# A third pair of up tiles by products of quarters, first in each of the last three passes of the MLP

## Chip, cores and metric

The kernel runs on 1 core of one Trainium2 chip. The metric is the device time of one execution in microseconds (us), as the median of several runs.

## The reference

Two decoder layers on a float32 input of 512 tokens by 1024 features. Each layer adds a mixer (four token mixers on one normalised input, gated and projected) and then an MLP:

```
for l in range(DEPTH):                       # DEPTH = 2
    h = rms_norm(x, ln_mix[l])
    x = x + hybrid_mixer(h, ...)             # not touched here
    h = rms_norm(x, ln_mlp[l])
    x = x + square(relu(h @ w_up[l])) @ w_down[l]   # 1024 -> 4096 -> 1024
```

## The kernel before

All products are float32 products made of three TensorE matmuls (`mm3`, line 268): each operand is split into a rounded part (`hi`) and the rest (`lo`), and hi·hi, hi·lo and lo·hi are added in PSUM. Activations are split once per layer. Weights come from one packed array in DRAM and are split as they arrive (`split_w`, line 258): ScalarE writes `whi`, VectorE writes `wlo`, into three rotating buffers each, so that a split may run three uses ahead of the matmuls.

The **MLP** (`mlp`, line 389) runs once per layer. Its 32 tiles of 128 columns of `w_up` are worked in four **passes** of eight (`PASSES`). In a pass, `t` runs from 0 to 3; each `t` makes one **pair** of up tiles, 256 hidden columns for all 512 tokens. A pair is made in one of two ways:

- **plain**: two weight tiles of 128x1024 through `next_w` (one load of 512 KB into a `raw` buffer, of which there are two, one split), each multiplied with all tokens: 2 tiles x 8 steps x 3 = 48 matmuls of 512 columns, into two PSUM banks of the kind `mm`;
- **by quarters** (`up_seven`, line 417), for the `t` listed in `SEVEN` for the pass: the pair is treated as a 2x2 block product, made with seven block products in place of eight (Winograd's form of Strassen's scheme). Four quarter weights B11, B12, B22, B21 of 256 KB each are loaded by SyncE's queue (line 426) into halves of four `cr` buffers; VectorE forms S1w = B11 + B12, S2w = S1w + B22, S3w = B12 + B22 and all4 = S2w + B21 in other halves of them; the four buffers `R[0..3]` are split as one each; then 7 forms x 4 steps x 3 = 84 matmuls of 256 columns go into four PSUM banks of the kind `ms`, in the order A, B, C, E, with small sums and copies between the forms. The sums of the activations (`sh`, `sl`) are made once per layer.

After each pair, ScalarE and VectorE form seven combinations of it (`ah`, `al`) for the second half of the pass, the **down products**, which are by quarters too: two groups of banks, `A`, `B` of the kind `mm` and `C`, `E` of the kind `ms` (E is ms2 and ms3). Their order on TensorE is A11 and S1, then S2, S4 (by k), S3, and at the end A22 and A12 by turns for k = 0, 1: A22 goes to E, A12 to A. When A22 of k = 1 is done, VectorE takes E out (`c21`, lines 708 to 713, two subtractions of 512 columns into `co`), while TensorE does the last A12. `turn.update(mm=2, ms=2)` (line 637) sets which banks come next: the next plain pair begins with mm2, the next pair by quarters with ms2.

The **six `cr` buffers** (`CRB`) serve the quarters of both halves: `chain` (2, W11 + W12 of the down weights, held to the end of the pass), `b22` (2) and `sum2` (2) in the down products, and four for each pair by quarters. A buffer goes to the next claimant when its last reader is done, so the quarters of the next pass are loaded while the down products still run. In passes 0 to 2 the results are added up in DRAM (`keep`), by SyncE's queue in pass 0 and by GpSimd's after it.

Nothing is ordered by hand beyond this. A scheduler puts the instructions of each engine in a fixed order before the run, by priority (weights and evictions are raised above the rest) and by its own estimate of when each is ready. On the chip each engine takes its instructions in that order.

Of the kernel before, what the change touches and what calls it, by code (L numbers as in the profile page):

```python
# [34 lines left out]
G1K = ((1, 1, 2, 2, 2), (2, 2, 2, 2))  # L35
KORD = ((0, 1, 2, 3, 4, 5, 6, 7), (4, 5, 6, 7, 0, 1, 2, 3))
PASSES = (8, 8, 8, 8)
SEVEN = ((2, 3), (2, 3), (2, 3), (2,))
CRB = 6
BIG = 1e30  # L40

# [12 lines left out]
def chunk_plan(l):  # L54
# [30 lines left out]
    for p, nt in enumerate(PASSES):  # L85

        half = nt // 2 * P
        for t in range(0, half, P):
            parts = 2 if t // P in SEVEN[p] else 1
            for i in range(parts):  # L90
# [80 lines left out]
def trunk(tc, x_in, wall, consts, lps, sgus, out):  # L171
# [5 lines left out]
    with ExitStack() as es:  # L177
# [14 lines left out]
        def mmtile(name, tag="mm", bank=None):  # L192
            if bank is None:
                bank = turn[tag]
                turn[tag] = (bank + 1) % 4
            return psum.tile([P, 512], F32, name=name, tag=f"{tag}{bank}")
# [49 lines left out]
        def next_w(raw=None):  # L246
            kk, n = chunk_shape(plan[pos[0]])
            pos[0] += 1
            L = kk * n
            if raw is None:  # L250
                raw = wpool.tile([P, WCH], F32, name="raw", tag="raw", bufs=WB[0])
            src = wall[off[0]:off[0] + P * L].rearrange("(p l) -> p l", l=L)
            off[0] += P * L
            with HP():
                nc.sync.dma_start(raw[:, :L], src)
            return split_w(raw, L, n, V.tensor_copy if pos[0] == 1 else S.copy)

        def split_w(raw, L, n, copy=S.copy):
            hi = wpool.tile([P, WCH], F32R, name="whi", tag="whi", bufs=WB[1])
            lo = wpool.tile([P, WCH], F32R, name="wlo", tag="wlo", bufs=WB[1])  # L260
            with HP():
                copy(hi[:, :L], raw[:, :L])
                r = V.tensor_sub(lo[:, :L], raw[:, :L], hi[:, :L].bitcast(F32))
            at["first"] = r if pos[0] == 1 else None
            return (hi[:, :L].rearrange("p (k n) -> p k n", n=n),
                    lo[:, :L].rearrange("p (k n) -> p k n", n=n))

        def mm3(o, ah, al, bh, bl, start, stop, more=False):

            T_.matmul(o, ah, bh, start=start, stop=False, skip_group_check=more)  # L270
            T_.matmul(o, ah, bl, start=False, stop=False, skip_group_check=more)
            r = T_.matmul(o, al, bh, start=False, stop=stop, skip_group_check=more)
            if not at["side"]:
                at["mm"] = r
# [11 lines left out]
        def tick():  # L286
            at["side"] = True
            for g in list(side):
                if next(g, side) is side:
                    side.remove(g)  # L290
            at["side"] = False
# [97 lines left out]
        def mlp(l, hh, hl, r2, gain, fp, sh, sl):  # L389
# [10 lines left out]
            with tc.tile_pool(name="ap", bufs=1) as ap:  # L400
                def ftile(name, tag):
                    return ap.tile([P, 7, 256], F32R, name=name, tag=tag)
# [4 lines left out]
                def cr():  # L407
                    return ap.tile([P, 1024], F32, name="cr", tag="cr", bufs=CRB)

                def moving(f, k):  # L410

                    if f >= S3:
                        return sh[k][:, f - S3], sl[k][:, f - S3]
                    k, r = k + 4 * (f in (A22, A12)), (row2, row1)[f in (A11, A12)]
                    return hh[k][:, r], hl[k][:, r]

                def up_seven(F):

                    base, sz = off[0], P * 512
                    off[0] += 4 * sz  # L420
                    pos[0] += 4

                    def ld(dst, i, j):
                        o = base + ((i - 1) * 2 + j - 1) * sz
                        with HP():
                            nc.sync.dma_start(dst, wall[o:o + sz].rearrange("(p l) -> p l", l=512))

                    R = [cr() for _ in range(4)]
                    R[1:] = R[2:] + R[1:2]
                    lo, up = slice(0, 512), slice(512, 1024)  # L430
                    B11, S1w, S2w, B22 = R[0][:, lo], R[0][:, up], R[1][:, lo], R[1][:, up]
                    S3w, all4, B21, B12 = R[2][:, lo], R[2][:, up], R[3][:, lo], R[3][:, up]
                    ld(B11, 1, 1)
                    ld(B12, 1, 2)
                    ld(B22, 2, 2)
                    ld(B21, 2, 1)
                    sums = {0: ((S1w, B11, B12),), 1: ((S2w, S1w, B22),), 2: ((S3w, B12, B22), (all4, S2w, B21)), 3: ()}
                    ws = [None] * 4

                    def form(f, o, i, n, first=True):  # L440
                        if ws[i] is None:
                            for o_, a_, b_ in sums[i]:
                                with HP():
                                    V.tensor_add(o_, a_, b_)
                            ws[i] = split_w(R[i], 512 if i == 3 else 1024, P)
                        w_h, w_l = ws[i]
                        for k in range(4):
                            bh, bl = moving(f, k)
                            mm3(o, w_h[:, 4 * n + k], w_l[:, 4 * n + k], bh, bl, first and k == 0, k == 3, not first)
                        tick()  # L450

                    A, B, C, E = (mmtile("up", "ms")[:, 0:256] for _ in range(4))
                    s1, s2 = (hpool.tile([P, 2, 256], F32, name="U", tag=n) for n in ("acc", "sq"))
                    U, U2, W, R5 = s1[:, 0], s1[:, 1], s2[:, 0], s2[:, 1]
                    form(A11, A, 0, 0)
                    with HP():
                        S.copy(U, A)
                    form(S1, B, 0, 1)
                    with HP():
                        S.copy(R5, B)  # L460
                    form(S2, C, 1, 0)
                    with HP():
                        V.tensor_sub(U2, C, U)
                    form(S4, B, 1, 1, False)
                    with HP():
                        V.tensor_add(F[:, A12], B, U2)
                    form(S3, C, 2, 0, False)
                    with HP():
                        V.tensor_sub(W, C, U)
                        V.tensor_add(F[:, A22], W, R5)  # L470
                        S.activation(F[:, 2:4], F[:, 2:4], AF.Relu)
                    form(A22, E, 2, 1)
                    with HP():
                        V.tensor_sub(F[:, A21], E, W)
                        S.activation(F[:, A21], F[:, A21], AF.Relu)
                    form(A12, A, 3, 0, False)
                    with HP():
                        S.activation(F[:, A11], A, AF.Relu)
                        S.activation(F, F, AF.Square)

                for p, nt in enumerate(PASSES):
                    nk = nt // 2
                    ah, al = [], []
                    for t in range(nk):
                        F = ap.tile([P, 4, 256], F32, name="F", tag="F")
                        G_ = ap.tile([P, 4, 256], F32, name="Fs", tag="Fs")
                        ah.append(ftile("ah", f"ah{t}"))
                        al.append(ftile("al", f"al{t}"))
                        if t == 1:
                            early = at["mm"]  # L490
                        if t in SEVEN[p]:
                            up_seven(F)
                        for i in range(0 if t in SEVEN[p] else 2):
                            w_h, w_l = next_w()
                            pt = mmtile("up")
                            fm_group(pt, w_h, w_l, hh, hl)
                            a = flat(F[:, 2 * i:2 * i + 2])
                            with HP():
                                S.activation(a, pt, AF.Relu)
                                S.activation(a, a, AF.Square)  # L500
                        with HP():
                            S.copy(ah[t][:, 0:3], F[:, 1:4])
                            V.tensor_sub(G_[:, 0:2], F[:, A21:A21 + 1].to_broadcast([P, 2, 256]), F[:, A11:A22 + 1])
                            V.tensor_sub(G_[:, 2], F[:, A11], G_[:, 1])
                            V.tensor_sub(G_[:, 3], F[:, A12], G_[:, 2])
                            S.copy(ah[t][:, 3:7], G_)
                            V.tensor_sub(al[t][:, 0:3], F[:, 1:4], ah[t][:, 0:3].bitcast(F32))
                            V.tensor_sub(al[t][:, 3:7], G_, ah[t][:, 3:7].bitcast(F32))
# [1096 lines left out]
```

## Time and profile before

| | us |
|---|---|
| median of 3 runs | 1582.65 (1582.23 to 1583.69) |
| the profiled execution, its own time | 1581.15 |
| its span, first to last instruction | 1579.4 |
| TensorE busy in the span | 1571.7 |
| VectorE busy | 1220.8 |
| ScalarE busy | 754.6 |

In the profile PE is TensorE's matmuls, PEld its weight loads, DVE is VectorE, ACT is ScalarE, POOL is GpSimd, SP is SyncE's queue. Times of rows are us from the span's start. Matmuls overlap in their pipeline: the step from one start to the next is what a matmul costs, and not the duration in its row. The granted clock is 1.0 of full speed in all slices of the span. The first layer's MLP runs from 461 to about 790 us, the second's from 1246 to the end.

### The profile page before, as it was taken

The numbers are of one execution on the slowest core, as the hardware profiler recorded it, in microseconds if no ns is written. First come the engines' busy times: TensorE is split into PE (matmuls) and PEld (weight loads), VectorE is DVE, ScalarE is ACT, GpSimd is POOL, SyncE is SP. The second block draws the span as 40 slices with busy tenths as digits, with TensorE's granted clock in tenths as the row PEclk, the third lists the DMA queues.
The fourth block names the chain that finished last, engine by engine and source line by source line (L and its number), as shares of the span: only waits on it lengthen the run. The fifth ranks groups of instructions, "written<-read, shape, count | busy, mean of one in ns | idle before, by whom it ended". The sixth has DMA issues, their size and how long they took to land.

```text
span 1579.4 us, 21779 instructions
## 1 busy us (share of the span) xinstructions
PE 1571.7 (100%) x8091; PEld 1319.1 (84%) x8091; DVE 1220.8 (77%) x2103; ACT 754.6 (48%) x1164; POOL 144.7 (9%) x189
## 2 busy tenths in 40 slices
PE   9999999999999999999999999999999999999998
PEld 8888888888888898988888888887888898989887
DVE  6899997645588787775978999975555896868677
ACT  5553224423356464746645433254233574737463
POOL 1322000000001011111013120000000010111110
PEclk9999999999999999999999999999999999999999
DMA  7533322332346466769445232223223565576692
GB/s 194 144 92 111 102 90 95 103 115 91 106 157 196 161 179 132 201 140 271 130 130 141 86 118 95 86 99 137 83 98 113 167 165 181 162 166 181 147 280 81
DMA packets 77835, 218.22 MB, mean 138 GB/s; under 512 B 8832, under 2 KB 16192, under 8 KB 77728
## 3 DMA queue, kind: packets, MB, share of 16 engines
q1 hardware_dynamic: 60784, 175.54, 33.8%
q0 software_dynamic: 16080, 40.27, 13.2%
q8 instruction: 64, 1.05, 0.3%
q10 hardware_dynamic: 864, 1.01, 0.2%
q14 instruction: 43, 0.35, 0.1%
HBM read 192.10 MB, written 21.01 MB: 135 GB/s over the span
## 4 chain that ended last, share of the span: by engine, by line
PE 91%; DVE 5%; DMA 2%; issue 1%; ACT 1%; SPq 0%; POOL 0%; DVEq 0%; ACTq 0%; POOLq 0%
PE g L143 21%; PE up L143 20%; PE tk L143 10%; PE q L143 10%; PE fm L143 8%; PE r L143 6%; PE p L143 5%; PE wo L143 4%; DVE wlo L143 2%; DMA cr<-in_wall_dram 1%; PE ix L143 1%; PE lg L143 1%; PE av L143 1%; PE pT L143 1%; DVE cr L143 0%
## 5 line engine op out<-in xcount | busy, mean ns | idle before, releaser
L143 ACT CAST whi<-raw 128x1024 fp32r<-128x1024 f32 (+3 forms) x208 | 228.6, 1099 | 217.4 <-DMA raw<-in_wall_dram 89.7
L143 DVE TENSOR_TENSOR wlo<-raw,whi 128x1024 fp32r<-128x1024 f32 (+3 forms) x209 | 267.8, 1282 | 80.0 <-ACT whi L143 79.6
L143 PE MATMUL g<-hh,whi 128*128 128x512 f32 x512 | 200.7, 392 | 0.0
L143 PE MATMUL g<-hh,wlo 128*128 128x512 f32 x512 | 199.7, 390 | 0.0
L143 PE MATMUL g<-hl,whi 128*128 128x512 f32 x512 | 199.5, 390 | 0.0
L143 DVE TENSOR_TENSOR wlo<-cr,whi 128x1024 fp32r<-128x1024 f32 (+1 forms) x136 | 157.8, 1165 | 45.1 <-ACT whi L143 44.9
L143 ACT CAST whi<-cr 128x1024 fp32r<-128x1024 f32 (+1 forms) x136 | 136.0, 1006 | 93.5 <-PE up L143 38.6
L143 PE MATMUL up<-hh,whi 128*128 128x512 f32 (+1 forms) x456 | 160.6, 352 | 0.0
L143 PE MATMUL up<-hh,wlo 128*128 128x512 f32 (+1 forms) x456 | 160.0, 351 | 0.4 <-DVE wlo L143 0.3
L143 PE MATMUL up<-hl,whi 128*128 128x512 f32 (+1 forms) x456 | 159.8, 350 | 0.0
L143 ACT ACTIVATE gs<-gs 128x512 f32<-128x512 f32 x64 | 40.6, 634 | 199.4 <-DVE gs L143 199.2
L143 PEld LDWEIGHTS g<-hh,wlo 128*128 128x128 f32 x512 | 96.1, 188 | 20.3
L143 PEld LDWEIGHTS g<-hh,whi 128*128 128x128 f32 x512 | 96.2, 188 | 19.5
L143 PEld LDWEIGHTS g<-hl,whi 128*128 128x128 f32 x512 | 96.2, 188 | 19.4
L143 PE MATMUL tk<-whi,hh 128*128 128x512 f32 (+2 forms) x304 | 107.9, 358 | 0.0
L143 PE MATMUL tk<-wlo,hh 128*128 128x512 f32 (+2 forms) x304 | 107.0, 354 | 0.2 <-DVE wlo L143 0.2
L143 PE MATMUL tk<-whi,hl 128*128 128x512 f32 (+2 forms) x304 | 106.5, 353 | 0.0
L143 DVE TENSOR_TENSOR gs<-g,rb 128x512 f32<-128x512 f32 x64 | 44.0, 688 | 78.8 <-PE g L143 78.7
L143 PE MATMUL q<-whi,ah 128*128 128x512 f32 (+1 forms) x260 | 100.5, 390 | 0.0
L143 PE MATMUL q<-whi,al 128*128 128x512 f32 (+1 forms) x260 | 100.0, 390 | 0.0
L143 PE MATMUL q<-wlo,ah 128*128 128x512 f32 (+1 forms) x260 | 99.6, 387 | 0.0
L143 PEld LDWEIGHTS up<-hh,wlo 128*128 128x128 f32 x456 | 86.3, 189 | 12.5 <-DVE wlo L143 1.3
(310 smaller groups left out, 3550.6 us busy)
## 6 DMA issues: line engine op xcount, KB each, us to landing
raw<-in_wall_dram SPq DMA_DIRECT2D x135, 512.0 KB, 3.7
raw<-in_wall_dram SPq DMA_DIRECT2D x64, 640.0 KB, 3.9
cr<-in_wall_dram POOLq DMA_DIRECT2D x48, 512.0 KB, 8.2
cr<-in_wall_dram SPq DMA_DIRECT2D x32, 512.0 KB, 5.1
cr<-in_wall_dram SPq DMA_DIRECT2D x56, 256.0 KB, 2.9
sum_dram<-co POOLq DMA_DIRECT2D x32, 256.0 KB, 5.8
x<-in_x_dram SPq DMA_DIRECT2D x16, 256.0 KB, 4.8
xm_dram<-x SPq DMA_DIRECT2D x16, 256.0 KB, 2.0
```

The costliest lines, as they stand in the source:

```text
L143: r = f(*a, **k)
```

## The change

```diff
-SEVEN = ((2, 3), (2, 3), (2, 3), (2,))
+SEVEN = ((2, 3), (0, 2, 3), (0, 2, 3), (0, 2))
...
-                def up_seven(F):
+                def up_seven(F, first):
...
                     R = [cr() for _ in range(4)]
-                    R[1:] = R[2:] + R[1:2]
+
+                    R = [R[2], R[0], R[1], R[3]] if first else [R[0], R[2], R[3], R[1]]
...
                         if t in SEVEN[p]:
-                            up_seven(F)
+                            up_seven(F, t == 0)
```

In passes 1, 2 and 3 of both layers the pair `t` = 0 is made by quarters in place of plain: six pairs in all. For these six the four `cr` buffers take other parts: of the four in the order in which they are claimed, the third holds B11 and S1w, the first S2w and B22, the second S3w and all4, the fourth B21 and B12. For all other pairs by quarters the parts are as before: first B11 and S1w, second B21 and B12, third S2w and B22, fourth S3w and all4. The packing of the weights follows `SEVEN`, so the DRAM array holds the four quarters of these pairs one after another. The bytes loaded per pair are the same, 1 MB.

## Rows read from the trace of the kernel before

**Rows 1.** The page: busy time of the engines with share of the span and count, and the chain of work that ended last, by engine.

```profile
PE 1571.7 (100%) x8091; PEld 1319.1 (84%) x8091; DVE 1220.8 (77%) x2103; ACT 754.6 (48%) x1164; POOL 144.7 (9%) x189
PE 91%; DVE 5%; DMA 2%; issue 1%; ACT 1%; SPq 0%; POOL 0%; DVEq 0%; ACTq 0%; POOLq 0%
```

**Rows 2.** Timeline of PE, layer 0, pass 3: the first matmul of the plain pairs 0 and 1, of the pair by quarters, of the plain pair behind it, and of the down products. Columns: start us, duration us, engine, line, operation, output and operands, shape.

```profile
705.03 0.39 PE L143 MATMUL up<-hh,whi 128*128 128x512 f32 x1
...
726.79 0.28 PE L143 MATMUL up<-hh,whi 128*128 128x256 f32 x1
726.91 0.28 PE L143 MATMUL up<-hl,whi 128*128 128x256 f32 x1
727.03 0.28 PE L143 MATMUL up<-hh,wlo 128*128 128x256 f32 x1
...
736.87 0.40 PE L143 MATMUL up<-hh,whi 128*128 128x512 f32 x1
737.10 0.40 PE L143 MATMUL up<-hl,whi 128*128 128x512 f32 x1
...
747.77 0.39 PE L143 MATMUL q<-whi,ah 128*128 128x512 f32 x1
```

**Rows 3.** The same starts in layer 1, pass 3.

```profile
1488.81 0.39 PE L143 MATMUL up<-hh,whi 128*128 128x512 f32 x1
...
1510.57 0.28 PE L143 MATMUL up<-hh,whi 128*128 128x256 f32 x1
...
1520.64 0.40 PE L143 MATMUL up<-hh,whi 128*128 128x512 f32 x1
```

**Rows 4.** Timeline of PE at the head of pass 2 (layer 0, then layer 1): the first three matmuls of the plain pair 0, and the first of the pair by quarters that ends the two plain pairs; the bracket is idle time before the instruction and its releaser.

```profile
623.94 0.39 PE L143 MATMUL up<-hh,whi 128*128 128x512 f32 x1
624.17 0.39 PE L143 MATMUL up<-hl,whi 128*128 128x512 f32 x1
624.89 0.50 PE L143 MATMUL up<-hh,wlo 128*128 128x512 f32 x1 [0.33 <-DVE wlo L143]
...
646.35 0.28 PE L143 MATMUL up<-hh,whi 128*128 128x256 f32 x1
...
1407.93 0.39 PE L143 MATMUL up<-hh,whi 128*128 128x512 f32 x1
...
1430.13 0.28 PE L143 MATMUL up<-hh,whi 128*128 128x256 f32 x1
```

**Rows 5.** Groups of instructions by shape while TensorE works on the pair by quarters of pass 3, layer 0 (726.79 to 736.87 us): count, busy us, mean ns of one. Neighbouring work of the engines is among them.

```profile
L143 DVE TENSOR_TENSOR wlo<-raw,whi 128x1024 fp32r<-128x1024 f32 x2 | 2.4, 1221 | 0.3 <-ACT whi L143 0.3
L143 ACT CAST whi<-raw 128x1024 fp32r<-128x1024 f32 x2 | 2.1, 1052 | 2.0 <-PE up L143 2.0
L143 DVE TENSOR_TENSOR U<-up,U 128x256 f32<-128x256 f32 x2 | 0.8, 418 | 0.0
L143 DVE TENSOR_TENSOR F<-up,U 128x256 f32<-128x256 f32 x2 | 0.8, 416 | 0.0
L143 DVE TENSOR_TENSOR wlo<-cr,whi 128x512 fp32r<-128x512 f32 x1 | 0.7, 683 | 0.0
L143 DVE TENSOR_TENSOR F<-U 128x256 f32<-128x256 f32 x1 | 0.4, 424 | 0.0
```

**Rows 6.** Busy time of the engines by stage, layer 0: down products of pass 1, then pass 2: the two plain pairs, the two pairs by quarters, the down products. Columns: stretch, its us, then busy us (count) of PE, PEld, DVE, ACT, POOL, granted clock, mean busy share of the DMA engines, GB/s.

```profile
585.65:623.94 38.29, 38.29 (x170) 31.40 (x169) 31.12 (x36) 18.85 (x23) 4.29 (x5) 1.00 0.66 161
623.94:646.35 22.41, 22.08 (x98) 17.95 (x96) 12.35 (x15) 11.40 (x16) 3.46 (x4) 1.00 0.65 153
646.35:666.73 20.38, 20.38 (x170) 20.21 (x168) 18.84 (x30) 15.24 (x23) 3.82 (x6) 1.00 0.76 201
666.73:705.03 38.30, 38.30 (x170) 31.40 (x169) 32.73 (x38) 20.07 (x25) 5.91 (x7) 1.00 0.64 154
```

**Rows 7.** Timeline of DVE around the head of pass 2, layer 0 (the pass begins at 623.94): sums of the next pass's quarters (cr<-cr), splits (wlo), and the two subtractions that take E out (co<-r,Z).

```profile
607.07 1.22 DVE L143 TENSOR_TENSOR wlo<-cr,whi 128x1024 fp32r<-128x1024 f32 x1
...
610.05 1.89 DVE L143 TENSOR_TENSOR cr<-cr 128x512 f32<-128x512 f32 x3
...
615.39 1.22 DVE L143 TENSOR_TENSOR wlo<-cr,whi 128x1024 fp32r<-128x1024 f32 x1
617.07 1.23 DVE L143 TENSOR_TENSOR wlo<-raw,whi 128x1024 fp32r<-128x1024 f32 x1 [0.46 <-ACT whi L143]
623.00 0.69 DVE L143 TENSOR_TENSOR cr<-cr 128x512 f32<-128x512 f32 x1 [4.71 <-DMA cr<-in_wall_dram]
623.61 1.22 DVE L143 TENSOR_TENSOR wlo<-raw,whi 128x1024 fp32r<-128x1024 f32 x1
624.75 1.28 DVE L143 TENSOR_TENSOR co<-r,Z 128x512 f32<-128x512 f32 x2
```

**Rows 8.** The same place in layer 1, and at the head of pass 1 in layer 0 and layer 1 (these begin at 543.51 and 1327.51), E's subtractions and the sum before them.

```profile
1406.77 0.69 DVE L143 TENSOR_TENSOR cr<-cr 128x512 f32<-128x512 f32 x1 [4.49 <-DMA cr<-in_wall_dram]
...
1408.52 1.28 DVE L143 TENSOR_TENSOR co<-r,Z 128x512 f32<-128x512 f32 x2
...
541.46 0.69 DVE L143 TENSOR_TENSOR cr<-cr 128x512 f32<-128x512 f32 x1 [3.60 <-DMA cr<-in_wall_dram]
543.21 1.28 DVE L143 TENSOR_TENSOR co<-r,Z 128x512 f32<-128x512 f32 x2
...
1323.42 0.69 DVE L143 TENSOR_TENSOR cr<-cr 128x512 f32<-128x512 f32 x1 [1.55 <-DMA cr<-in_wall_dram]
...
1325.16 1.28 DVE L143 TENSOR_TENSOR co<-r,Z 128x512 f32<-128x512 f32 x2
```

**Rows 9.** Timeline of DVE at the head of pass 3, layer 0 (it begins at 705.03): no sum of quarters stands there.

```profile
698.16 1.22 DVE L143 TENSOR_TENSOR wlo<-raw,whi 128x1024 fp32r<-128x1024 f32 x1 [0.46 <-ACT whi L143]
700.88 1.22 DVE L143 TENSOR_TENSOR wlo<-raw,whi 128x1024 fp32r<-128x1024 f32 x1 [1.50 <-ACT whi L143]
702.02 1.28 DVE L143 TENSOR_TENSOR co<-r,Z 128x512 f32<-128x512 f32 x2
```

**Rows 10.** SP's queue: the loads of quarters during the down products of pass 1, layer 0; and, over the whole run, from issue to landing of these loads.

```profile
597.70 0.33 SPq L426 DMA_DIRECT2D cr<-in_wall_dram  x1
602.36 8.13 SPq L426 DMA_DIRECT2D cr<-in_wall_dram  x4
...
616.64 0.83 SPq L426 DMA_DIRECT2D cr<-in_wall_dram  x2
DMA to landing us min/median/max: 2.4/2.9/8.2
```

## The prediction

> **What bounds the kernel now.** I read the page first. TensorE is busy for 1571.7 of the span's 1579.4 us and carries 91% of the chain that ended last; VectorE follows with 77%, ScalarE with 48% [rows 1]. A chain of that kind is shortened by taking matmul time away, if nothing new keeps TensorE waiting. A busy matmul row is not yet a price, since matmuls overlap, so next I read starts in TensorE's timeline: from the head of a pair to the head of the next one [rows 2, 3]. Then the heads of the passes, where the change puts its work: TensorE's waits there [rows 4], what VectorE has in hand [rows 7 to 9], and what loads run [rows 10]. Last, busy time by stage, for whether VectorE can carry the new work [rows 6].
>
> **What is removed and added on TensorE.** A plain pair costs (726.79 - 705.03) / 2 = 10.88 us, that is 48 steps of 0.227 [rows 2]. A pair by quarters between plain ones costs 736.87 - 726.79 = 10.08 us, 84 steps of 0.120 [rows 2]; in layer 1 it is (1510.57 - 1488.81) / 2 = 10.88 against 10.07 [rows 3]. So a quarter step is more than half a plain step, and of the eighth of the columns that the scheme saves (84 x 256 against 48 x 512) only 0.80 us of 10.88 is left. The new pair also has a plain pair behind it, so I take the 10.08. Six pairs: 6 x 0.80 = **4.8 us less**, 0.30% of the run.
>
> **VectorE, ScalarE.** A plain pair asks VectorE for two splits, 2 x 1.22 = 2.4 us. A pair by quarters asks for four sums of 0.69 (the row at 623.00 in [rows 7]), three splits of 1.22, one of 0.68, and five small operations of 0.42 [rows 5]: 2.8 + 4.3 + 2.1 = 9.2. So each new pair adds 6.8 us to VectorE. On the path it would be ruinous. I cost it at nothing, since this is its cover: in pass 2 VectorE is busy 12.35 of 22.41 us in the two plain pairs and 18.84 of 20.38 in those by quarters [rows 6]; with 6.8 more, 38.0 of about 42, still under the time, and part of it (sums, the first split) falls into the down products before, where 31.12 of 38.29 are used. If that cover is gone, the price is the overhang of VectorE over TensorE. ScalarE, at 11.40 of 22.41 [rows 6], gets 1.7 casts of 1.05 [rows 5] and some small copies: nothing. The quarters' own evictions run in the existing pairs without a wait that I can see in their 10.08 us.
>
> **Loads and queues.** Two loads of 512 KB become four of 256 KB on SP's queue: the same bytes, two more issues of 0.33 [rows 10]. What matters is when buffers come free. The loads of quarters in pass 1's down products start at 597.70, four from 602.36 to 610.5, and two at 616.64 [rows 10]: I read this as the first pair by quarters getting the buffers of b22 and sum2, which are done early, and the second one those of chain, of which the last is held by the split at 615.39 to 616.61 [rows 7]. After the change the new pair gets the early four. With its exchanged parts, its sums wait for the fourth, freed when the split at 607.07 ends, about 608.3 [rows 7]; with the median landing of 2.9 us [rows 10] they can start at about 611.2, and the first split is wanted at 623.94, 12 us later. With the longest landing, 8.2, it is still 7 us early. I cost this at nothing. On SP, what waits behind these loads are the raw loads of the pair after (needed 10 us later than today) and in pass 0 the stores of sums, which nobody waits for. GpSimd's queue is passed by nothing.
>
> **The heads of the passes: what goes and what comes.** Today the head of pass 2 loses 22.41 - 21.76 = 0.65 us in layer 0 and (1430.13 - 1407.93) - 21.76 = 0.44 in layer 1: the third matmul waits for a wlo [rows 4], and that is late because VectorE stood 4.71 us before a sum whose quarter had not landed, with the ready split behind it [rows 7]. This sum belongs to the second pair by quarters of the coming pass, 22 us before its use.
>
> The change adds one wait here. The plain pair begins in bank mm2; the new pair begins in ms2, which is half of E. Its first form cannot start before VectorE's first subtraction on E is over; behind that form stands the whole of TensorE. Undisturbed, that subtraction is early: at pass 3 the two run from 702.02 to 703.30, the first done at about 702.66, 2.4 us before the head [rows 9]. Behind a stalled sum it is late: 624.75 + 0.64 = 625.39, 1.45 after the head of pass 2; 1408.52 + 0.64 is 1.23 after it in layer 1; in pass 1 0.35 after it in layer 0 (543.85), and 1.7 before it in layer 1 (1325.80) [rows 7, 8]. No row shows pass 3 with such a sum: bounds 0 [rows 9] and 1.45 [rows 7].
>
> Does the stalled sum still stand ahead of E's subtraction? The next pair in line for the two late buffers is then `t` = 2, so a sum of the same kind can stand there, its load issued at the same moment. But that order is the scheduler's, by its estimate of readiness, and VectorE now has the new pair's four sums, which come earlier in the program and so take precedence, in the same stretch (from 611 on, where three such sums stood at 610.05 [rows 7]); E's subtraction also takes precedence over the stray sum once both are ready. I hold it a little likelier that the sum falls behind. Bounds of the new waits together: 0, and 5.7 if all is as today (0.35 + 1.45 + 0 + 1.23, and 2 x 1.34 for pass 3, the mean of 1.45 and 1.23). I take 0.7, two heads at the smallest late row, being nearer to the undisturbed row.
>
> The row at 623.00 shows VectorE idle with ready work behind a blocked instruction. The Trainium skill, PSUM — Partial Sum Buffer, section Engine vs sequencer instructions, says that ScalarE's and VectorE's queues are strictly first in, first out, and this row agrees. The rule speaks against the change: by it any late quarter ahead of E's subtraction holds TensorE itself, which is the second case below; by the sum above it would not.
>
> **The sum.** Old stalls gone 1.1, matmul time 4.8, new waits 0.7: 5.2 us less. Against the profiled execution, 1581.15 - 5.2 = 1575.95; the median of three runs stands 1.5 us above that execution, so on it 1582.65 - 5.2 = **1577.5**. What the measurement can tell from no change is about 0.2%, or 3.2 us.
>
> **The rivals.**
> 1. *Forecast.* E is out before the head in most passes. With new waits of 0 to 2.7 us: 1576.7 to 1579.4. Chance 0.48.
> 2. *The wait moves instead of going.* The stray sum stays ahead of E's subtraction; the 5.7 us of waits above replace the 1.1 and eat the gain: 1582.65 - 5.9 + 5.7 = **1582.4**, from 1579.5 to 1585 as landings vary. For it: four heads of four have the sum ahead today (541.46, 623.00, 1323.42, 1406.77 [rows 7, 8]). Against it: the fuller VectorE. Chance 0.35.
> 3. *Slower.* One mechanism, same place: at the heads the first form waits for E, E's subtraction for a sum, the sum for a quarter that lands later than today, since the new pair's loads are in flight too. The landing of 623.00 was 6.3 us after its issue at 616.64; the longest in the run is 8.2 [rows 10], so a head can lose 1.45 + 1.9 = 3.35 us, and six lose 20: 1597. It makes the kernel slower from (5.9 + 3.2) / 6 = 1.5 us a head; at 2.5 a head it gives 1582.65 - 5.9 + 15 = **1591.8**. Against it: the DMA engines' mean share there is 0.65 [rows 6], and the bytes are the same. Chance 0.14.
> 4. *The short matmuls run at half the plain step.* Then the pair costs 84 x 0.1134 = 9.52 and six save 8.2: 1582.65 - 8.2 - 0.4 = **1574.0**. The rows speak against it, 0.120 in both layers [rows 2, 3]. Chance 0.03. The Trainium skill, TensorE: Matmul & The Clock Gate, section Back-to-back issue gap, gives N/2.4 + 2.5 ns for a lone warm matmul, 109 ns at 256 columns and 216 at 512; an estimate by that page would save 1.2 us a pair, 7.1 in all. The trace differs, 120 and 227, and decides.
>
> That the change does not do what it says is no case: `SEVEN` alone chooses, and matmuls of 256 columns must grow by 6 x 84.
>
> **How the numbers follow.** Predicted is the first case. The range takes in cases 1 and 2 nearly whole, from 1576.2 (no new wait, less the 0.4 us by which the lowest run lies below the median) to 1584.5; outside lie case 3, case 4 and a little of case 2. Faster by over 0.2% (under 1579.5): cases 1 and 4 and a little of 2, 0.53. Slower (over 1585.8): case 3 and a shade more, 0.15. Within: 0.32. The forecast's own range is 1576.2 to 1579.4.
>
> **What would show it.** Right: `t` = 0 of passes 1 to 3 takes 10.1 us from its first to the next pair's first matmul; E's subtractions end before the heads; no wait of TensorE there. Case 2 or 3: the first matmul of 256 columns in a pass starts 0.3 to 3 us late with VectorE's co as releaser, and VectorE waits for cr from DMA ahead of it. If `t` = 0 is longer without a late start, VectorE has no room and the cover above was wrong. If waits appear in pairs 2 and 3, the exchange of buffers has made their loads late, which I have costed at nothing.

## The result and the profile after

The changed kernel is slower: 1596.18 us median (1593.51 to 1598.97, 4 runs) against 1582.67 (4 runs), a ratio of 1.0082 with a 95% interval of 1.0068 to 1.0097. The profiled execution took 1595.87 us with a span of 1594.1, both 14.7 us more than before (1581.15 and 1579.4). Forecast was 1577.5 in a range up to 1584.5; the time lies outside, where the prediction had put a chance of 0.15.

The page of the changed kernel, busy time and chain by engine, beside [rows 1]:

```profile
PE 1572.3 (99%) x8307; PEld 1326.3 (83%) x8307; DVE 1259.0 (79%) x2169; ACT 766.9 (48%) x1188; POOL 145.1 (9%) x189
PE 72%; DVE 12%; issue 6%; DMA 6%; ACT 2%; POOL 1%; SPq 0%; DVEq 0%; ACTq 0%; POOLq 0%
```

PE is still 99% busy by that row. What changed is the chain: TensorE carries 72% of it in place of 91, VectorE 12 in place of 5, DMA 6 in place of 2. So I read where TensorE waited. Waits of PE over the whole span, in total, times, longest:

```profile
PE up L143 <- ACT U L143: 4.9, 5, 1.3
PE up L143 <- DVE co L143: 4.0, 3, 2.1
PE up L143 <- DVE wlo L143: 3.1, 2, 1.9
PE up L143 <- ACT whi L143: 2.3, 2, 1.2
```

That is 14.3 us. The same view of the kernel before has only two rows of up tiles, 0.9 us in all, the first of them in pass 0:

```profile
PE up L143 <- DVE U L143: 0.6, 1, 0.6
PE up L143 <- DVE wlo L143: 0.3, 1, 0.3
```

The new waits lie at three places of a pass. Timeline of PE of the changed kernel, layer 0, pass 2: the first form of the new pair, its fourth form, the plain pair 1, and a stretch behind it; then the heads of pass 1 and 3 in layer 0, and of pass 1 in layer 1.

```profile
626.39 0.36 PE L143 MATMUL up<-hh,whi 128*128 128x256 f32 x1 [1.14 <-ACT whi L143]
...
632.21 0.39 PE L143 MATMUL up<-sh,whi 128*128 128x256 f32 x1 [1.27 <-ACT U L143]
...
640.54 0.50 PE L143 MATMUL up<-hh,wlo 128*128 128x512 f32 x1 [1.85 <-DVE wlo L143]
...
642.99 0.63 PE L143 MATMUL up<-hh,whi 128*128 128x512 f32 x1
643.41 0.63 PE L143 MATMUL up<-hl,whi 128*128 128x512 f32 x1
...
544.70 0.36 PE L143 MATMUL up<-hh,whi 128*128 128x256 f32 x1 [0.32 <-DVE co L143]
...
713.12 0.36 PE L143 MATMUL up<-hh,whi 128*128 128x256 f32 x1 [1.54 <-DVE co L143]
...
1337.15 0.28 PE L143 MATMUL up<-hh,whi 128*128 128x256 f32 x1
...
1347.23 0.40 PE L143 MATMUL up<-hh,whi 128*128 128x512 f32 x1
```

Undisturbed, in pass 1 of layer 1, the new pair takes 1347.23 - 1337.15 = 10.08 us, the forecast price of [rows 2]. Elsewhere it is late. The table goes by the starts of neighbouring matmuls in the same view (a start less the start before it, less one step):

| place | us late, layer 0 passes 1, 2, 3 | layer 1 | sum |
|---|---|---|---|
| first form of the new pair | 0.48, 1.29, 1.69 | 0, 1.33, 2.27 | 7.1 |
| fourth form (S4), with slow steps around it | 0.7, 1.5, 1.4 | 0, 1.4, 1.4 | 6.4 |
| plain pair 1 | 0, 3.8, 0 | 0, 1.5, 0 | 5.3 |
| slow steps at heads, start of pass 3's down products | | | 1.5 |

That is 20.3 us; with 4.8 saved on matmuls and 1.1 of old waits gone, it makes 14.4 beside the 14.7 us measured. Two differences outside these places are not in that sum and cancel in part: the first up matmul starts 1.5 us later (462.98 in place of 461.44), and 0.8 us is gone with the wait in pass 0.

VectorE of the changed kernel at the head of pass 2, layer 0, to set against [rows 7], and on into pair 1 (on time the pass would begin at 625.10, which is 626.39 less the 1.29 of the table):

```profile
618.22 1.23 DVE L143 TENSOR_TENSOR wlo<-raw,whi 128x1024 fp32r<-128x1024 f32 x1 [0.45 <-ACT whi L143]
623.82 0.69 DVE L143 TENSOR_TENSOR cr<-cr 128x512 f32<-128x512 f32 x1 [4.37 <-DMA cr<-in_wall_dram]
624.43 1.22 DVE L143 TENSOR_TENSOR wlo<-cr,whi 128x1024 fp32r<-128x1024 f32 x1
625.57 1.28 DVE L143 TENSOR_TENSOR co<-r,Z 128x512 f32<-128x512 f32 x2
626.76 1.21 DVE L143 TENSOR_TENSOR wlo<-cr,whi 128x1024 fp32r<-128x1024 f32 x1
628.37 1.90 DVE L143 TENSOR_TENSOR cr<-cr 128x512 f32<-128x512 f32 x3 [0.39 <-DMA cr<-in_wall_dram]
...
638.33 0.69 DVE L143 TENSOR_TENSOR cr<-cr 128x512 f32<-128x512 f32 x1 [3.96 <-DMA cr<-in_wall_dram]
638.94 0.42 DVE L143 TENSOR_TENSOR U<-up,U 128x256 f32<-128x256 f32 x1
639.27 1.22 DVE L143 TENSOR_TENSOR wlo<-raw,whi 128x1024 fp32r<-128x1024 f32 x1
```

The stray sum, that of a later pair, is still there (623.82), for pair 2, with 4.37 us of idle time before it. E's first subtraction ends at about 625.57 + 0.64 = 626.21 and the first form starts at 626.39, though PE's row names ScalarE's whi: the cast that ended last before it (625.29 + 1.04 = 626.33, next view) is of a split that the first form does not read; its own was cast at 619.85. At the heads where no cast falls there (544.70, 713.12 above) the row names VectorE's co. A second stray sum, for pair 3, stands at 638.33 ahead of the split that pair 1 wants; TensorE's matmul of 640.54 comes behind that split.

ScalarE of the changed kernel at the same place: casts, the two evictions of the last down product (co<-q), and the copies (U<-up) that the fourth form needs.

```profile
619.85 1.05 ACT L143 CAST whi<-cr 128x1024 fp32r<-128x1024 f32 x1 [1.67 <-PE q L143]
...
623.93 0.59 ACT L143 COPY co<-q 128x512 f32<-128x512 f32 x1 [0.30 <-PE q L143]
625.29 1.04 ACT L143 CAST whi<-cr 128x1024 fp32r<-128x1024 f32 x1 [0.77 <-PE q L143]
630.51 0.59 ACT L143 COPY co<-q 128x512 f32<-128x512 f32 x1 [4.17 <-DMA sum_dram<-co]
630.99 0.38 ACT L143 COPY U<-up 128x256 f32<-128x256 f32 x1
...
631.77 0.39 ACT L143 COPY U<-up 128x256 f32<-128x256 f32 x1
```

The second eviction waits 4.17 us for its result buffer, until an earlier result has been stored; the two copies stand behind it, and the fourth form starts at 632.21 when the second copy is over. With three buffers that earlier result is E's first half, whose store starts when its subtraction is done. In the kernel before the same eviction waited for a store too, with no matmul behind it that needed such copies:

```profile
631.44 0.59 ACT L143 COPY co<-q 128x512 f32<-128x512 f32 x1 [2.17 <-DMA sum_dram<-co]
```

### The profile page after: what moved, and what is told of

Read it like the earlier page. It is cut to its first block, busy times and chain, and to the rows that moved or that the text cites. A ratio compares the mean times of both kernels' runs of the same rounds, so it can differ in the third digit from the quotient of the medians.

```text
span 1594.1 us, 22365 instructions
## 1 busy us (share of the span) xinstructions
PE 1572.3 (99%) x8307; PEld 1326.3 (83%) x8307; DVE 1259.0 (79%) x2169; ACT 766.9 (48%) x1188; POOL 145.1 (9%) x189
## 4 chain that ended last, share of the span: by engine, by line
PE 72%; DVE 12%; issue 6%; DMA 6%; ACT 2%; POOL 1%; SPq 0%; DVEq 0%; ACTq 0%; POOLq 0%
PE g L143 17%; PE up L143 15%; PE tk L143 8%; PE q L143 8%; PE fm L143 6%; PE wo L143 5%; PE p L143 4%; PE r L143 4%; DVE wlo L143 4%; DMA cr<-in_wall_dram 3%; DVE sco L143 2%; DMA raw<-in_wall_dram 2%; ACT whi L143 1%; DMA sum_dram<-co 1%; DVE m L143 1%
## 5 line engine op out<-in xcount | busy, mean ns | idle before, releaser
L143 ACT CAST whi<-raw 128x1024 fp32r<-128x1024 f32 (+3 forms) x196 | 215.8, 1102 | 173.7 <-DMA raw<-in_wall_dram 36.5
L143 DVE TENSOR_TENSOR wlo<-raw,whi 128x1024 fp32r<-128x1024 f32 (+3 forms) x197 | 253.0, 1285 | 34.3 <-ACT whi L143 33.1
L143 ACT CAST whi<-cr 128x1024 fp32r<-128x1024 f32 (+1 forms) x160 | 158.7, 997 | 114.6 <-PE r L143 43.7
L143 DVE TENSOR_TENSOR wlo<-cr,whi 128x1024 fp32r<-128x1024 f32 (+1 forms) x160 | 183.7, 1153 | 37.4 <-ACT whi L143 36.9
L143 PE MATMUL up<-hh,whi 128*128 128x256 f32 (+1 forms) x432 | 144.6, 335 | 6.3 <-DVE co L143 4.0
L143 PE MATMUL up<-hh,wlo 128*128 128x256 f32 (+1 forms) x432 | 143.5, 332 | 3.1 <-DVE wlo L143 3.1
L143 PE MATMUL up<-hl,whi 128*128 128x256 f32 (+1 forms) x432 | 143.2, 332 | 0.0
L143 PEld LDWEIGHTS g<-hh,wlo 128*128 128x128 f32 x512 | 96.1, 188 | 20.3
L143 DVE TENSOR_TENSOR cr<-cr 128x512 f32<-128x512 f32 (+1 forms) x96 | 71.8, 776 | 47.7 <-DMA cr<-in_wall_dram 47.4
```

Source lines behind the costliest of these rows:

```text
L143: r = f(*a, **k)
```

## The experiments

My theory after this reading is one cause: in VectorE's fixed order the sums of later pairs stand ahead of urgent work and wait for quarters that land late; ScalarE's delay follows from E's late exit. The rivals are that VectorE has no room for the new pair, the claim on E's bank, the result buffer, and the place at the head. Open besides is what makes the quarters late. Ratios are to the kernel before as run beside each experiment (medians 1583.2 to 1583.5).

**e1: both stray sums held back.**

```diff
-    V.tensor_add(o_, a_, b_)
+    r = V.tensor_add(o_, a_, b_)
+if gate is not None:     # order for the scheduler alone
+    tc.add_manual_dep(ins_of(r), ins_of(gate).name, V._dep, reason="pace")
...
+    heads.append(at["mm"])          # last matmul before pair t
-    up_seven(F, t == 0)
+    up_seven(F, t == 0, heads[t - 2] if t > 1 else None)
```

> The changed kernel, with one ordering rule for the scheduler: the sums of quarters of pair 2 come only after the last matmul of the pass before, those of pair 3 only after the last matmul of pair 0. Loads, splits, banks and matmuls are as in the changed kernel. My theory: in the fixed order of VectorE a sum of a later pair stands ahead of work that TensorE needs now, at the head of the pass (the sum at 623.82) and again in the plain pair 1 (the sum at 638.33), and waits there for a quarter that lands late; ScalarE's late copies at the head are a consequence (E's results leave late, so their stores end late and the last eviction of the down products waits for its buffer). Then nearly all of the 20 us of waits goes: 1576 to 1580 us. Rival, VectorE has no room: the same work in another order still takes as long, 1592 or more. Rival, the bank: E's half is claimed too early whatever VectorE's order, 1588 or more.

Measured: 1580.45 us (10 runs), ratio to before 0.9977 (0.9968 to 0.9987). VectorE in this run at the head of pass 2, layer 0:

```profile
621.41 1.23 DVE L143 TENSOR_TENSOR wlo<-cr,whi 128x1024 fp32r<-128x1024 f32 x1 [1.50 <-ACT whi L143]
622.55 1.28 DVE L143 TENSOR_TENSOR co<-r,Z 128x512 f32<-128x512 f32 x2
624.13 1.22 DVE L143 TENSOR_TENSOR wlo<-cr,whi 128x1024 fp32r<-128x1024 f32 x1 [0.29 <-ACT whi L143]
625.27 0.68 DVE L143 TENSOR_TENSOR cr<-cr 128x512 f32<-128x512 f32 x1
626.59 1.29 DVE L143 TENSOR_TENSOR cr<-cr 128x512 f32<-128x512 f32 x2 [0.63 <-DMA cr<-in_wall_dram]
```

The pass begins on time at 625.56, and E's first subtraction starts 3.0 us ahead of that; in the changed kernel it started 0.5 us behind it (625.57 against 625.10). Of the waits in the new pairs and in pair 1 only the fourth form's are left, 0.4, 0.5, 1.3 and 0.4 us. The time is 0.45 us above the range that I had given. The same operations in another order take 16 us less, so VectorE has the room; the order was the cause of most of it. The bank's rival falls too: E's half is still claimed first. But ScalarE's delay does not follow from E's late exit alone: 2.5 us of it stay with E on time, and e5 removes them.

**e2: only pair 2's sums held back** (`heads[0] if t == 2 else None`).

> As the run before, but only the sums of pair 2 are held back; the early sum of pair 3 stays where it is. My theory: the waits at the heads and at the fourth form (about 14 us) go, those in pair 1 of the two passes with three pairs by quarters (about 5 us with the slower clock behind one of them) stay: 1580 to 1586 us. If the waits in pair 1 came only from the late heads, they go as well and the time is that of the run before.

Measured: 1583.05 us (10 runs), ratio 0.9994 (0.9984 to 1.0003). The late matmul of pair 1 in pass 2, layer 0 and then layer 1:

```profile
636.78 0.50 PE L143 MATMUL up<-hh,wlo 128*128 128x512 f32 x1 [1.16 <-DVE wlo L143]
...
1419.90 0.50 PE L143 MATMUL up<-hh,wlo 128*128 128x512 f32 x1 [0.41 <-DVE wlo L143]
```

By starts it is late by 1.33 us in layer 0 and 0.57 in layer 1; in the changed kernel pair 1 lost 3.8 and 1.5. So the sum of pair 3 is a cause of its own, about 2 us here (the medians of e2 and e1 lie 2.6 apart), and the larger part of what pair 1 lost, the slower clock behind it included, goes with the sums of pair 2.

**e3: another bank.**

```diff
-turn.update(mm=2, ms=2)
+turn.update(mm=2, ms=0 if p < last else 2)
```

> The changed kernel with one number changed: in passes 0 to 2 the next pair by quarters begins with bank ms0 (free since the product S3) in place of ms2 (half of E). Nothing else moves. If the claim on E's bank is the cause, the 7 us of late heads go and the fourth form is on time: 1585 to 1590 us. My theory: the third matmul of the first form then waits for the first split, which stands behind the same stalled sum and ends only 0.6 us before E's first subtraction does, and the later waits stay: 1592 to 1596 us.

Measured: 1598.02 us (4 runs), ratio 1.0088 (1.0073 to 1.0103): nothing gained, and 2 us above the range of my theory. PE at the head of pass 2, layer 0, and at the fourth form:

```profile
624.00 0.28 PE L143 MATMUL up<-hh,whi 128*128 128x256 f32 x1
...
624.98 0.39 PE L143 MATMUL up<-hh,wlo 128*128 128x256 f32 x1 [0.58 <-DVE wlo L143]
...
631.48 0.39 PE L143 MATMUL up<-sh,whi 128*128 128x256 f32 x1 [2.16 <-ACT U L143]
```

The first matmul is on time, the third waits for the split behind the stray sum (late by 0.74, 0.95, 0.94, 1.59 us in passes 2 and 3), and the fourth form, late by 1.3 or 1.4 us before, is late by 2.0 to 2.4. The wait that I had forecast, E's bank, was only the first of several in a row on the same late sum.

**e4: a fourth result buffer.**

```diff
-n = at["co"] = (at["co"] + 1) % 3
+n = at["co"] = (at["co"] + 1) % 4
...
```

> The changed kernel with a fourth result buffer for the down products (three before), and a narrower table of constants that makes room for it. The last eviction by ScalarE then need not wait for a store, so the copies behind it that the fourth form needs are early. Heads and pair 1 are untouched. If ScalarE's wait is a cause by itself, 5 to 6 us go: 1589 to 1592 us. If something else is just as late there (VectorE's split of the second buffer, at 627.97), the gain is 0 to 2 us: 1594 to 1597.

Measured: 1594.91 us (4 runs), ratio 1.0070 (1.0053 to 1.0088). Pair 1 of pass 2, layer 0:

```profile
640.89 0.63 PE L143 MATMUL up<-hh,wlo 128*128 128x512 f32 x1 [2.81 <-DVE wlo L143]
```

The waits for ScalarE's copies are gone (the fourth form is late by at most 0.4 us), yet this matmul of pair 1 is now late by 2.97 and 3.00 us in the two layers. Counted from the head's due time it starts about 15.5 us later in both kernels (640.54 - 625.10; 640.89 - 625.42). What is saved ahead of a stray sum is lost at it.

**e5: sums held back and the fourth buffer** (e1 and e4 together).

> Both pairs' sums held back as in the first experiment, and the fourth result buffer. What is left in the first experiment are waits of the fourth form for ScalarE's copy (0.4, 0.4, 1.3, 0.3 us) that stands behind the eviction of the down products, which waits for its buffer. If that is all, they go: 1577 to 1579 us, the new pair takes 10.1 to 10.2 us at all six places. If the fourth form then waits for something else as late, the time stays at 1580.

Measured: 1578.49 us (1577.68 to 1579.72, 6 runs), ratio 0.9966 (0.9954 to 0.9979). Timeline of PE in this run, pass 2, layer 0, the first matmul of the new pair and of pair 1:

```profile
624.50 0.28 PE L143 MATMUL up<-hh,whi 128*128 128x256 f32 x1
...
634.57 0.40 PE L143 MATMUL up<-hh,whi 128*128 128x512 f32 x1
```

That is 10.07 us, as at four more of the six places; the sixth takes 10.24. The result buffer is thus a cause of its own, worth about 2 us beside e1. This version beats both kernels.

**e6: the third pair at t = 1** (`SEVEN = ((2, 3), (1, 2, 3), (1, 2, 3), (1, 2))`).

> The changed kernel with the third pair by quarters at t = 1 in place of t = 0 (three in a row before the down products), no sums held back. If the price was the place at the head (E's bank, late evictions of the pass before), the heads are as before the change and the time is 1577 to 1581 us. My theory gives VectorE's order the blame: sums of later pairs still stand ahead of work in hand, and with three pairs by quarters in a row VectorE has 11.6 us of work for each 10.1 of TensorE, so 1581 to 1590 us, with the waits inside pairs 1 to 3.

Measured: 1604.75 us, ratio 1.0134 (1.0119 to 1.0149), worse than either theory had it. VectorE in this run, pass 2, layer 0:

```profile
629.20 1.23 DVE L143 TENSOR_TENSOR wlo<-cr,whi 128x1024 fp32r<-128x1024 f32 x1
638.99 0.69 DVE L143 TENSOR_TENSOR cr<-cr 128x512 f32<-128x512 f32 x1 [8.56 <-DMA cr<-in_wall_dram]
```

So the loss does not need the place at the head; away from it a sum waits 8.56 us. I took VectorE's load for the price here and was wrong in that: what the row shows is again a wait for a quarter, only longer. Its load is issued at 630.46, and four transfers that add results into DRAM are in flight beside it. Whether three pairs in a row would fit with their sums held back was not tried.

**e7: the kernel before, with sums held back** (the edit of e1 without the new pairs).

> The kernel before, with the sums of pair 2 held back until the last matmul of the pass before, those of pair 3 until the last matmul of pair 0; no new pair. It shows what holding back is worth by itself: my theory says only the 1.1 us of waits at the heads of pass 2, 1581 to 1582 us. If holding back gained more than that in the first experiment's way (3 us or more here), the new pair would not be what is gained there.

Measured: 1581.83 us (10 runs), ratio 0.9989 (0.9980 to 0.9998). Holding back is worth about a thousandth without the new pairs; between e7 and e5 lie 3.3 us. These 3.3 us are not the gain of the new pairs as it stands. In the profiled executions e5 reaches its first up matmul 1.25 us later than e7 (463.60 and 462.35), in a part where the two do not differ. From there to the first down product of pass 3 it takes 282.52 and 282.66 us in the two layers and e7 285.81 and 284.83, together 5.5 less. 1.0 of this is a wait in pass 0 that e7 has and e5 has not, so 4.5 are left beside the 4.8 forecast. What moves the start between runs was not looked into.

**e8 and e10: why the quarters land late.** Just before the late quarters are loaded, GpSimd stores `c22`, one of the four results of the down products, as two transfers of 256 KB that add to what is in DRAM. In e8 this store is left out in passes 1 and 2; in e10 it overwrites in place of adding. The output of both lacks the parts in question.

```diff
 def keep(i, tok, f, tiles):
+    if p > 0 and i == 1:                                # e8
+        return
...
+        if p > 0 and i == 1:                            # e10
+            nc.gpsimd.dma_start(dst, tiles[b])
...
```

> The changed kernel without one of the four stores of results (c22) in passes 1 and 2 of both layers, so its output lacks those parts. These stores, added up in DRAM, are issued by GpSimd about 1.5 us before the loads of the quarters that land late (616.32 and 617.79 at the head of pass 2). If they make the landing late (6.0 us from issue), the wait of the sum at the heads of passes 2 and 3 shrinks from 4.4 to 5.4 us to 1 to 2, as at the head of pass 1 in layer 1, and TensorE's late starts there go. If the two raw loads of 512 KB in flight are the cause, the wait stays above 3 us.

> The changed kernel with the stores of result c22 in passes 1 and 2 written over what is in DRAM in place of added to it (same bytes, same queue, same place in the order; the sum in DRAM lacks the earlier passes there). If it is the adding that holds up the quarters' loads, the sum at the heads of passes 2 and 3 waits 1 to 2.5 us in place of 4.4 to 5.4 and the time falls to 1582 to 1588. If any store of 512 KB there does it, nothing changes: 1593 to 1599.

Measured, one execution each: 1582.81 and 1582.56 us. The stray sum at the head of pass 2, layer 0, first in e8:

```profile
620.51 0.69 DVE L143 TENSOR_TENSOR cr<-cr 128x512 f32<-128x512 f32 x1 [1.08 <-DMA cr<-in_wall_dram]
621.12 1.22 DVE L143 TENSOR_TENSOR wlo<-cr,whi 128x1024 fp32r<-128x1024 f32 x1
622.25 1.28 DVE L143 TENSOR_TENSOR co<-r,Z 128x512 f32<-128x512 f32 x2
```

and in e10:

```profile
620.94 0.69 DVE L143 TENSOR_TENSOR cr<-cr 128x512 f32<-128x512 f32 x1 [1.53 <-DMA cr<-in_wall_dram]
```

The order is the same, the loads are issued at the same time, and the sum waits 1.1 and 1.5 us in place of 4.4. Over the four heads of passes 2 and 3 it waits 4.4 to 5.4 us in the changed kernel, 1.1 to 1.4 in e8, and in e10 1.3 to 1.5 at three of them but 3.32 at the fourth, the head of pass 3 in layer 1. So it is mostly the adding of c22 into DRAM, not the bytes of its store nor the raw loads, that holds up the quarters in flight beside it. It is not the only thing: at the head of pass 1 in layer 0 no such store is in flight, and the sum waits 3.56 us in the changed kernel and 3.43 in e8. What is slow there, and at the fourth head of e10, is open. Both edits also free result buffers sooner, so the 13 us are not the sum's alone.

**e9: the exchange of buffers undone** (`R = [R[0], R[2], R[3], R[1]]` for all).

> The changed kernel with the exchange of the four quarter buffers undone for the new pairs (all pairs use the order of before). The prediction counted on the exchange to make the new pair's sums later. The trace after the change shows these sums at the times of before (one at 606.96, three at 611.21), so I now expect that the exchange only renames buffers: 1593 to 1599 us, the same as the changed kernel. If it matters, the time moves by over 4 us either way.

Measured: 1596.36 us (4 runs), ratio 1.0085 (1.0068 to 1.0102), the changed kernel's time. The exchange makes no difference that the time shows.

## Why the prediction was wrong, step by step

- **The price on TensorE held.** 10.08 us forecast, 10.07 or 10.08 measured wherever nothing waits.
- **The steps that failed** are all in one term of the sum, "new waits 0.7": it measured 20.3 us, 18.8 of them at three places.
- **First, the choice at the heads**, "I hold it a little likelier that the sum falls behind". It did not; all six heads have the sum first. I argued from precedence among ready work; no run shows why the scheduler put it first, but the four heads of four that I had put beside the second rival were the better evidence. The second rival's size was near: 5.7 us of late first forms forecast, 7.1 measured. With these alone the time would have been about 1584, still inside the range. What took it outside are the next two, which the sum did not hold.
- **Second, ScalarE at "nothing"**, with the words that the quarters' own evictions run without a wait: 6.4 us at the fourth form. I looked at ScalarE's busy time, which is no guide to who stands behind a blocked instruction; and of E's late exit I priced the first reader (the bank), not the store and the buffer behind it.
- **Third, pair 1**, 5.3 us in two passes. I saw the stray sum at the head only. With three pairs by quarters the next pair's sum meets the plain pair's splits, 13 us on.
- **The third rival** named the place and the direction rightly (late quarter, sum, E, first form), but not its reason nor its size. The quarter lands no later than in the kernel before: at the head of pass 2 in layer 0 the sum starts 6.4 us after the issue of [rows 10] there and 6.0 here (617.79 to 623.82), and it starts no later after its issue at the three other heads that have it in both kernels. The heads lost 1.2 us each, under its 1.5. That its 20 us for six heads, 1597, lie beside the measured 20.3 and 1596.18 is luck: two thirds of the waits are at places that it did not name.
- **The exchange of buffers** was read as moving the sums to 611. Three of the new pair's sums are at 611.21 but the first is at 606.96, in the same order as in the kernel before; e9 shows no effect. It cost nothing either way.
- **VectorE's cover held**: e5 carries the full work with 0.2 us lost in pairs 0 to 3 of passes 1 to 3.
- **Loads "on time"** was right for the new pair's own quarters; the late ones belong to the pairs behind it.

## What to carry to other kernels

On an engine that takes its work in a fixed order, an operation for later is not free because the engine is idle there. Price it by its longest wait and by what stands behind it, and hold it back until the urgent work is past. When a change makes TensorE need an eviction or a copy sooner, list all that is queued ahead of that on its engine, with what each of those waits for, down to stores and result buffers. Removing one of several waits that hang on the same late event gained nothing here (e3) or hardly anything (e4); find the event.

## What the hardware showed that I had not expected

- At the heads of passes 2 and 3 a store that adds into DRAM slowed the loads beside it. A pair of quarter loads issued at 617.79 let its sum start at 623.82 in the changed kernel; issued at 617.78 without that store it let the sum start at 620.51 (6.0 and 2.7 us), and with a plain store of the same bytes 3.2 us after issue. By the trace's landing times the first of these loads lands 0.17 to 0.21 us behind the second transfer of the adding store at all four heads of the changed kernel (623.72 behind 623.55 here).
- Behind the waits of pass 2 in layer 0 TensorE's granted clock fell from the upper level (2.4 GHz, 1.00) to the lower (1.2 GHz, 0.50). Busy time by stage of the changed kernel (columns as in [rows 6]):

```profile
641.50:644.50 3.00, 3.00 (x9) 2.33 (x8) 2.26 (x3) 2.97 (x5) 0.00 (x0) 0.50 0.80 214
```

Steps there are 0.42 us (642.99 to 643.41 above) in place of 0.23; ahead of it TensorE's matmuls had been late by 1.29, 1.43 and 2.02 us. About 1.7 of the 3.8 us of that pair are its price. In pass 2 of layer 1, late by 1.33, 1.31 and 1.43, it did not fall. In e8, in pass 2 of layer 1, it fell behind a single wait of 1.91 us, with none in the pair before it; the late matmul and, behind it, busy time by stage:

```profile
1420.91 0.50 PE L143 MATMUL up<-hh,wlo 128*128 128x512 f32 x1 [1.91 <-DVE wlo L143]
...
1422.00:1425.00 3.00, 3.00 (x9) 2.33 (x8) 2.26 (x3) 2.97 (x5) 0.00 (x0) 0.50 0.79 224
```

So the two earlier waits are not needed for the fall.
